# First feed-forward projection as Strassen products: seven half-width products for every two output pairs, and tile pools per phase

## The chip, the cores and the metric

The kernel runs on one core of a Trainium2 chip. The metric is device time in microseconds (us); 1770.32 us before the change is the median of three runs (1770.07 to 1771.31). The engines named below are TensorE (PE in the profile, with its weight loads as PEld), VectorE (DVE), ScalarE (ACT), GpSimd (POOL) and SyncE (SP), whose queue issues most loads.

## The reference

Two identical decoder layers on 512 tokens of width 1024, all in float32. A layer first adds the output of four causal token mixers (forgetting attention, gated linear attention, retention, a state-space scan) that share one input projection; then it adds a gated feed-forward block. The change lies in the latter:

```python
def swiglu(h, w_in, w_out):
    gate, up = jnp.split(h @ w_in, 2, axis=-1)
    return (jax.nn.silu(gate) * up) @ w_out

for l in range(DEPTH):                       # 2 layers
    h = rms_norm(x, ln1[l])
    x = x + mixer_block(h, ...)
    h = rms_norm(x, ln2[l])
    x = x + swiglu(h, w_ffn_in[l], w_ffn_out[l])
```

`w_ffn_in` is 1024 x 5632 (2816 gate columns, then 2816 up columns), `w_ffn_out` is 2816 x 1024.

## The kernel before

**Layout.** Activations are kept transposed: 128 features on the partitions, 512 tokens along the row. `x` has `KD` = 8 such tiles. The hidden width of 2816 is `NF` = 22 blocks of 128. A weight block is 128 x 128. A matmul takes a weight block as its stationary operand and 512 tokens as its moving one, and fills one PSUM bank of 128 x 512.

**Three passes.** Float32 accuracy comes from splitting every operand into a rounded high part (float32r) and a low part, what the rounding left. `mm3` (L164) issues three matmuls for one product: high by high, low weights by high moving, high weights by low moving. `split` (L175) makes the parts: a ScalarE copy rounds to the high part (L176), and a VectorE subtraction gives the low part (L177). All of these matmuls are recorded at L162.

**Weights.** They are packed on the host in the order of use, eight blocks to a slab of 128 x 1024 (512 KB). `load` puts a slab's transfer on SyncE's queue into `wr` (two buffers); `convert` splits it into `wh` and `wl` (three buffers each). `block` hands out the next block and calls `ahead`, which keeps `AHEAD` = 2 slabs prepared. In the program every slab is loaded once.

**Order.** The kernel is written in the Tile language: the program lists operations, and a scheduler places them on the engines' queues by a simulated timeline, with waits and buffer slots worked out from the data flow. An engine executes its own queue in order. In the mixers, pieces of the projections (`fill`) are mixed by hand with the mixers' own small matmuls. One pool `tp` of 37 tiles (128 x 512 float32, tag `t`) serves all temporary values of the whole kernel, in mixers and feed-forward alike.

**Feed-forward.** After the mixers' output projection, `resid` adds each result to `x` (L1155) and feeds the norm `n2`: `Norm.feed` makes the high and low part of `x` times the norm's gain, and sums of squares. The factor 1/rms per token, `n2.r`, is not in these parts; it is applied behind the projection. The block then runs in two halves (`hf`) of 11 blocks each. In the first half `group` computes the first two gate and up pairs, four columns at once in the four `mx` banks, while the last tiles of `x` come in; the other pairs come from `proj`, one column at a time, into four `mm` banks. `swiglu` multiplies gate and up by `n2.r` (L1175, L1176, VectorE), applies Silu (ScalarE), multiplies them (L1178, GpSimd) and splits the product. Then the half's 11 blocks go through `w_ffn_out`: four output columns together, then four one at a time, and `done` adds each to `x`: a plain addition after the first half (L1198), `resid` after the second, with the next layer's norm or the store of the output (L1159).

## Time and profile before

| what | value |
|---|---|
| median of three runs | 1770.32 us |
| profiled execution: its own time | 1771.39 us |
| profiled execution: span, first to last instruction | 1769.70 us |
| TensorE clock granted (mean) | 0.999 |
| instructions | 21568 |
| bytes moved by DMA | 163.31 MB |
| time share of DMA queue q1, all 16 engines | 27.5% |

The span is 1.69 us shorter than that execution's own time. Busy times in the profile are sums over an engine's instructions with overlaps counted once, except in the rows of groups, where each instruction counts in full: matmuls overlap there, since each one's time holds its latency, and the step from one start to the next is the shorter number. In rows of groups, `mm<-xh,wl` is a matmul into a `mm` bank with `xh` moving and `wl` stationary; `x128` is the count; behind the bar stand busy us, mean ns of one, and idle time ahead with its releaser.

### The profile page before, as it was taken

How to read it: one execution, taken by the hardware profiler on the slowest of the kernel's cores; microseconds unless marked ns; L12 is line 12 of the kernel's file. 1: busy time of each engine (PE TensorE's matmuls, PEld its weight loads, DVE VectorE, ACT ScalarE, POOL GpSimd, SP SyncE). 2: the span in 40 equal slices, each digit the busy share in tenths (PEclk: the TensorE clock that was granted, in tenths of full speed). 3: DMA queues.
4: the chain of work that ended last, by engine and by line, in shares of the span. 5: the costliest groups of instructions: out<-in, count | busy, mean ns of one | idle time of the engine just before them, and what ended most of it. 6: DMA issues, size and time to landing. Idle time of an engine off the chain costs nothing.

```text
span 1769.7 us, 21568 instructions
## 1 busy us (share of the span) xinstructions
PE 1760.0 (99%) x8700; PEld 1463.6 (83%) x8700; DVE 1041.5 (59%) x1427; ACT 684.8 (39%) x926; POOL 230.3 (13%) x210
## 2 busy tenths in 40 slices
PE   8999999999999999999999999999999999999999
PEld 7878888888888888888888788888888888888887
DVE  5866675777674443444447676867775644334442
ACT  5424543555443321223324254345554432223221
POOL 2032120022101110011000321201220111001100
PEclk9999999999999999999999999999999999999999
DMA  5322222222232222222323222222222323222222
GB/s 188 108 72 72 73 84 77 91 84 84 93 98 95 96 95 96 96 97 95 107 84 107 72 73 71 84 84 84 95 79 84 103 96 101 98 95 96 95 96 95
DMA packets 46036, 163.31 MB, mean 92 GB/s; under 512 B 5104, under 2 KB 5488, under 8 KB 45936
## 3 DMA queue, kind: packets, MB, share of 16 engines
q1 hardware_dynamic: 45072, 160.45, 27.5%
q10 hardware_dynamic: 864, 1.48, 0.3%
q8 instruction: 68, 1.11, 0.3%
q14 instruction: 32, 0.26, 0.1%
HBM read 159.81 MB, written 2.10 MB: 91 GB/s over the span
## 4 chain that ended last, share of the span: by engine, by line
PE 98%; ACT 0%; DVE 0%; DMA 0%; issue 0%; DVEq 0%; ACTq 0%
PE mm L162 83%; PE mx L162 14%; PE mx L1033 1%; DMA x<-in_x_dram 0%; PE mx L633 0%; DVE xl L355 0%; DVE t L367 0%; ACT xh L200 0%; ACT t L200 0%; PE mx L905 0%; PE mx L825 0%; DVE wl L177 0%; ACT wh L176 0%; ACT L195 0%; PE mx L621 0%
## 5 line engine op out<-in xcount | busy, mean ns | idle before, releaser
L176 ACT CAST wh<-wr 128x1024 fp32r<-128x1024 f32 (+1 forms) x300 | 313.1, 1045 | 737.8 <-PE mm L162 599.5
L162 PE MATMUL mm<-xh,wl 128*128 128x512 f32 x1504 | 589.2, 392 | 0.0
L162 PE MATMUL mm<-xh,wh 128*128 128x512 f32 x1504 | 589.1, 392 | 0.0
L162 PE MATMUL mm<-xl,wh 128*128 128x512 f32 x1504 | 588.1, 391 | 0.0
L177 DVE TENSOR_TENSOR wl<-wr,wh 128x1024 fp32r<-128x1024 f32 (+1 forms) x300 | 409.9, 1366 | 285.6 <-ACT wh L176 284.6
L162 PE MATMUL mm<-t,wh 128*128 128x512 f32 x1152 | 367.5, 390 | 0.0
L162 PEld LDWEIGHTS mm<-xh,wh 128*128 128x128 f32 x1504 | 282.5, 188 | 58.9 <-issue 1.3
L162 PEld LDWEIGHTS mm<-xl,wh 128*128 128x128 f32 x1504 | 282.5, 188 | 58.9 <-issue 1.3
L162 PEld LDWEIGHTS mm<-xh,wl 128*128 128x128 f32 x1504 | 282.6, 188 | 58.5 <-issue 1.1
L162 PEld LDWEIGHTS mm<-t,wh 128*128 128x128 f32 x1152 | 216.4, 188 | 44.7
L162 PE MATMUL mm<-t,wl 128*128 128x512 f32 x576 | 224.8, 390 | 0.0
L1178 POOL TENSOR_TENSOR t<-t,t 128x512 f32<-128x512 f32 x44 | 56.8, 1290 | 538.6 <-DVE t L1176 467.4
L162 PEld LDWEIGHTS mm<-t,wl 128*128 128x128 f32 x576 | 108.2, 188 | 22.0
L176 ACT CAST t<-t 128x512 fp32r<-128x512 f32 x112 | 68.7, 621 | 88.5 <-POOL t L1178 42.0
L177 DVE TENSOR_TENSOR t<-t,t 128x512 fp32r<-128x512 f32 x112 | 78.2, 704 | 29.6 <-ACT t L176 22.9
L1176 DVE TENSOR_TENSOR t<-mm,t 128x512 f32<-128x512 f32 x40 | 27.7, 691 | 115.0 <-PE mm L162 115.0
L200 ACT ACTIVATE t<-t 128x512 f32<-128x512 f32 x121 | 73.7, 628 | 24.2 <-DVE t L1175 14.5
L1126 POOL TENSOR_TENSOR t<-t,t 128x512 f32<-128x512 f32 x32 | 43.6, 1361 | 249.1 <-DVE t L1122 243.7
L162 PE MATMUL mx<-t,t 64*128 64x128 f32 (+6 forms) x576 | 63.8, 290 | 0.0
L1175 DVE TENSOR_TENSOR t<-mm,t 128x512 f32<-128x512 f32 x40 | 27.6, 691 | 61.1 <-PE mm L162 61.1
L162 PEld LDWEIGHTS mx<-t,t 128*128 128x128 f32 (+3 forms) x576 | 50.5, 165 | 14.2 <-issue 8.0
L162 PE MATMUL mx<-xh,wl 128*128 128x512 f32 x128 | 50.7, 400 | 3.0 <-DVE wl L177 3.0
(210 smaller groups left out, 1661.2 us busy)
## 6 DMA issues: line engine op xcount, KB each, us to landing
wr<-in_wst_dram SPq DMA_DIRECT2D x296, 512.0 KB, 3.3
out_dram<-x SPq DMA_DIRECT2D x8, 256.0 KB, 2.4
x<-in_x_dram SPq DMA_DIRECT2D x3, 512.0 KB, 6.3
wr<-in_wst_dram SPq DMA_DIRECT2D x4, 256.0 KB, 5.9
x<-in_x_dram SPq DMA_DIRECT2D x2, 256.0 KB, 5.4
cs<-in_cst_dram ACTq DMA_DIRECT2D x1, 462.0 KB, 5.9
pr<-in_par_dram ACTq DMA_DIRECT2D x2, 167.0 KB, 5.1
posi<-in_pos_dram ACTq DMA_DIRECT2D x1, 256.0 KB, 6.8
```

What stands on the lines that cost most here:

```text
L162: T.matmul(o, lhsT=l, rhs=r, start=start, stop=stop, skip_group_check=True)
L176: A.copy(out=hi, in_=src)
L177: V.tensor_tensor(out=lo, in0=src, in1=hi.bitcast(F32), op=ALU.subtract)
L200: i = A.activation(out=out, in_=in_, func=func, **kw)
L1033: T.transpose(ps[:, W:W + P], zs[qb][:, kb * P:(kb + 1) * P], ident)
L1126: (V if last else G).tensor_tensor(out=merged[d], in0=merged[d], in1=t, op=ALU.add)
L1175: V.tensor_tensor(out=a, in0=pg, in1=n2.r, op=ALU.mult)
L1176: V.tensor_tensor(out=u, in0=pu, in1=n2.r, op=ALU.mult)
L1178: G.tensor_tensor(out=a, in0=a, in1=u, op=ALU.mult)
```

## The change

The first projection of 20 of the 22 block pairs is computed by Strassen's scheme (in Winograd's form). A unit is two neighbouring blocks, each with its gate and its up column; for gate and up alike the 2 x 2 scheme runs over two output blocks, two halves of the contraction (`HK` = 4 tiles each) and two halves of the tokens (`H` = 256). Instead of eight quarter products there are seven, each 2 (gate, up) x 4 x 3 matmuls of 256 columns. They accumulate in three pairs of PSUM banks `a`, `b`, `c`, and ScalarE copies and VectorE sums (`collect`) put the four quarters of gate and up together.

The token sums t1 to t4 are made once per layer by `sums`, called inside the plain group that computes the first two pairs as before. The weight sums are made on the chip for every unit: `load` fetches four quarters (three into a new pool `rq`, one into `wr`), `prep` makes sums and splits three products ahead on VectorE and ScalarE. For three products that use a weight quarter as it is (`LATE`), the low part is made otherwise: ScalarE writes the negated rounded value, and an accumulating transfer on GpSimd's queue adds the weights from memory a second time (`early`).

The feed-forward block now runs in four parts (`PARTS` = 6, 6, 6, 4 blocks), each with its units and then its share of `w_ffn_out`. `swiglu` works on gate and up of two blocks at once (128 x 1024) and multiplies only the gate by `n2.r`; the up side's factor moves into `done`, which has two VectorE operations. The product of gate and up moves from GpSimd to VectorE. `mm3` issues high by high, high weights by low moving, low weights by high moving. Pools are opened and closed per phase: the mixers have 33 temporary tiles, the norms four of their own (`NT`), and the feed-forward phase its own pools in the same memory. `sbd` is cleared once per layer. `cap` keeps slabs from being prepared past the end of a phase.

The diff, cut to its core:

```diff
+    def mixers():
+        return phase(gp=2, vp=2, bd=1, tp=33)
...
     def mm3(o, l, r, start, stop):
         (lh, ll), (rh, rl) = l, r
         mm(o, lh, rh, start, False)
-        mm(o, ll, rh, False, False)
-        mm(o, lh, rl, False, stop)
+        mm(o, lh, rl, False, False)
+        mm(o, ll, rh, False, stop)
...
+        scope = phase(tq=1, ep=8, rp=5, lp=2, fp=9)
 
         last = l == DEPTH - 1
+        tb_ = {n: tuple(pools["tq"].tile([P, HK, H], F32R, tag=n + h, name=nm(n + h)) for h in "hl") for n in ("t1", "t2", "t3")}
+        tb_["t4"] = n2.hi[:, :HK, H:], n2.lo[:, :HK, H:]
+        tb_["b11"] = n2.hi[:, :HK, :H], n2.lo[:, :HK, :H]
+        tb_["b21"] = n2.hi[:, HK:, :H], n2.lo[:, HK:, :H]
+        tb_["b22"] = n2.hi[:, HK:, H:], n2.lo[:, HK:, H:]
+
...
+        def sums():
+            g = PR("ln2")
+            xg = []
+            for k in range(0, KD, 2):
+                t = FT([P, 2, S])
+                for i in range(2):
+                    act(out=t[:, i], in_=x[:, k + i], func=AF.Copy, scale=g[:, k + i:k + i + 1])
+                xg.append(t)
+            one_, two = slice(0, H), slice(H, S)
+
+            def make(n, f):
+                t = FT([P, HK, H])
+                for i in range(2):
+                    a, b = f(i)
+                    V.tensor_tensor(out=t[:, 2 * i:2 * i + 2], in0=a, in1=b, op=ALU.subtract)
+                split(t, *tb_[n])
+                return t
+
+            t1 = make("t1", lambda i: (xg[i][:, :, two], xg[i][:, :, one_]))
+            t2 = make("t2", lambda i: (xg[2 + i][:, :, two], t1[:, 2 * i:2 * i + 2]))
+            make("t3", lambda i: (xg[2 + i][:, :, two], xg[i][:, :, two]))
+            make("t4", lambda i: (xg[2 + i][:, :, one_], t2[:, 2 * i:2 * i + 2]))
+
+        RIGHT = {1: "b11", 2: "b21", 3: "b22", 4: "t4", 5: "t1", 6: "t2", 7: "t3"}
+        LATE = (1, 2, 4)
+        OF = {1: "11", 2: "12", 4: "22"}
+
+        def strassen(units):
+            n = len(units)
+            st = [{} for _ in units]
+            stream = [(0, 1), (0, 2)]
+            for u in range(n):
+                if u == n - 1 and u:
+                    stream += [(u, p) for p in (6, 5, 7, 2, 3, 4)]
+                else:
+                    stream += [(u, 6)] + ([(u, 2)] if u else []) + [(u, 5), (u, 7)]
+                    stream += [(u + 1, 1)] if u < n - 1 else []
+                    stream += [(u, 3), (u, 4)]
+            def load(u):
+                for q, (dk, dm) in (("11", (0, 0)), ("12", (HK, 0)), ("21", (0, 1)), ("22", (HK, 1))):
+                    if q == "22":
+                        t = wp.tile([P, SLAB * P], F32, tag="wr", name=nm("wr"), bufs=2)
+                    else:
+                        t = pools["rp"].tile([P, SLAB * P], F32, tag="rq", name=nm("rq"))
+                    j = len(qkeys) // SLAB
+                    for base in (0, FFN):
+                        qkeys.extend([("w_ffn_in", l, k + dk, base + (units[u] + dm) * P) for k in range(HK)])
+                    nc.sync.dma_start(out=t, in_=wsq[j])
+                    st[u][q] = t, j
+
+            def sub(o, a, b, op=ALU.subtract):
+                V.tensor_tensor(out=o, in0=a, in1=b, op=op)
+                return o
+
+            def LT():
+                return pools["lp"].tile([P, SLAB * P], F32R, tag="l", name=nm("l"))
+
+            def early(u, p):
+                t, j = st[u][OF[p]]
+                lo = wp.tile([P, SLAB * P], F32R, tag="wl", name=nm("wl"))
+                A.activation(out=lo, in_=t, func=AF.Copy, scale=-1.0)
+                G.dma_start(out=lo, in_=wsq[j], accum_op=ALU.add)
+                st[u]["lo", p] = lo
+
+            def prep(u, p):
+                s = st[u]
+                hi = wp.tile([P, SLAB * P], F32R, tag="wh", name=nm("wh"))
+                if p in LATE:
+                    A.copy(out=hi, in_=s[OF[p]][0])
+                    s[p] = hi, s.pop(("lo", p))
+                    return
+                a11, a12, a21, a22 = (s[q][0] for q in ("11", "12", "21", "22"))
+                if p == 6:
+                    s1 = wp.tile([P, SLAB * P], F32, tag="wr", name=nm("wr"), bufs=2)
+                    s["s1"] = sub(s1, a21, a22, ALU.add)
+                    sub(a21, a11, a21)
+                    sub(a11, s1, a11)
+                    s[p] = split(a11, hi, LT())
+                    if u + 1 < len(units):
+                        load(u + 1)
+                    return
+                if p == 3:
+                    sub(a12, a12, a11)
+                t = {5: s["s1"], 7: a21, 3: a12}[p]
+                s[p] = split(t, hi, LT())
+
...
+            def begin(i):
+                if i < 0:
+                    load(0)
+                    upto("early", 2, early, lambda p: p in LATE)
+                    return
+                upto("prep", i + 3, prep, lambda p: True)
+                upto("early", i + 6, early, lambda p: p in LATE)
+
+            def product(u, p):
+                s = st[u]
+                hi, lo = s.pop(p)
+                if p in (1, 2, 5):
+                    s["abc"[(1, 2, 5).index(p)]] = [MM(), MM()] if p == 1 else [MX(), MX()]
+                bank = s["b" if p == 2 else "c" if p in (3, 5) else "a"]
+                rh, rl = tb_[RIGHT[p]]
+                for g in range(2):
+                    for k in range(HK):
+                        sl = slice((HK * g + k) * P, (HK * g + k + 1) * P)
+                        mm3(bank[g][:, :H], (hi[:, sl], lo[:, sl]), (rh[:, k], rl[:, k]), p in (1, 2, 5) and k == 0, k == HK - 1)
+
+            def collect(u, p, have):
+                s = st[u]
+                left, right = slice(0, H), slice(H, S)
+
+                def copy(n):
+                    for g in range(2):
+                        s[n, g] = pools["ep"].tile([P, H], F32, tag="e", name=nm("e"))
+                        A.copy(out=s[n, g], in_=s["a"][g][:, :H])
+
+                def plus(n, bank, i, cols):
+                    for g in range(2):
+                        V.tensor_tensor(out=s["t"][g][:, i, cols], in0=s[bank][g][:, :H], in1=s.pop((n, g)), op=ALU.add)
+
+                if p in (1, 6, 7):
+                    copy({1: "e1", 6: "e2", 7: "e3"}[p])
+                if "t" not in s and p != 1:
+                    s["t"] = [FT([P, 2, S]), FT([P, 2, S])]
+                if p == 2:
+                    plus("e1", "b", 0, left)
+                if p == 7:
+                    plus("e3", "c", 1, right)
+                if p == 3:
+                    plus("e2", "c", 0, right)
+                if p == 4:
+                    for g in (1, 0):
+                        A.copy(out=s["t"][g][:, 1, left], in_=s["a"][g][:, :H])
+                    swiglu(*s.pop("t"))
+            def run():
+                for i, (u, p) in enumerate(stream):
+                    begin(i)
+                    if i >= len(stream) - 2:
+                        ahead(len(keys) // SLAB + AHEAD - len(stream) + 1 + i)
+                    product(u, p)
+                    collect(u, p, None)
+                assert done_["prep"] == len(stream)
+
...
+        def swiglu(a, u):
+            V.tensor_tensor(out=a, in0=a, in1=n2.r.unsqueeze(1).broadcast_to([P, 2, S]), op=ALU.mult)
+            act(out=a, in_=a, func=AF.Silu)
+            V.tensor_tensor(out=a, in0=a, in1=u, op=ALU.mult)
+            hi, lo = split(a, FT([P, 2, S], F32R), FT([P, 2, S], F32R))
+            acts.extend((hi[:, i], lo[:, i]) for i in range(2))
+
...
-            def swiglu(pg, pu):
-                a, u = TT(), TT()
-                V.tensor_tensor(out=a, in0=pg, in1=n2.r, op=ALU.mult)
-                V.tensor_tensor(out=u, in0=pu, in1=n2.r, op=ALU.mult)
-                act(out=a, in_=a, func=AF.Silu)
-                G.tensor_tensor(out=a, in0=a, in1=u, op=ALU.mult)
-                acts.append(split_tile(a))
...
+        def hook():
+            sums()
+            begin(-1)
+
+        ps4 = group("w_ffn_in", l, [0, FFN, P, FFN + P], n2, KD, hook)
...
+        for part, n in enumerate(PARTS):
+            end = part == len(PARTS) - 1
+            cap[0] = len(keys) // SLAB + n + (FRONT // SLAB if end and not last else 0)
+            run()
+            if end and not last:
                 o, w = PAR_OFF["ln1"]
                 nn = Norm(pr[:, l + 1, o:o + w])
+            k0 = sum(PARTS[:part])
 
             def done(ps, d):
-                if hf == 0:
-                    V.tensor_tensor(out=x[:, d], in0=ps, in1=x[:, d], op=ALU.add)
-                else:
-                    resid(ps, d, nn)
-
-            ps4 = [MM() for _ in range(4)]
-            for k in range(HF):
+                t = FT([P, 2, S])[:, 0]
+                V.tensor_tensor(out=t, in0=ps, in1=n2.r, op=ALU.mult)
+                V.tensor_tensor(out=x[:, d], in0=x[:, d], in1=t, op=ALU.add)
+                if end and not last:
+                    nn.feed(d)
+                elif end:
+                    nc.sync.dma_start(out=out[:, d], in_=x[:, d])
+
+            ps4 = [MX() for _ in range(4)]
+            for k in range(n):
                 for i in range(4):
-                    mm3(ps4[i], block("w_ffn_out", l, hf * HF + k, P * i), acts[k], k == 0, k == HF - 1)
+                    mm3(ps4[i], block("w_ffn_out", l, k0 + k, P * i), acts[k], k == 0, k == n - 1)
+            if not end:
+                begin, run = ready_for(part + 1)
+                begin(-1)
             for i in range(4):
                 done(ps4[i], i)
             for d in range(4, KD):
                 ps = MM()
-                for k in range(HF):
-                    mm3(ps, block("w_ffn_out", l, hf * HF + k, P * d), acts[k], k == 0, k == HF - 1)
+                for k in range(n):
+                    mm3(ps, block("w_ffn_out", l, k0 + k, P * d), acts[k], k == 0, k == n - 1)
                 done(ps, d)
+            acts.clear()
```

More of the change, by code (lines that the diff above doesn't have):

```diff
@@ L206, in trunk @@
     raw, ready = [], []
+    cap = [SLABS]
     def load():
@@ L257, in wide @@
         return hi[:, sl], lo[:, sl]
+    scope = mixers()
     x = cp.tile([P, KD, S], F32, name="x")
@@ L399, in proj, with layer @@
         return ps
-    def layer(l, n1):
+    def layer(l, n1, scope):
+        sbd = pools["bd"].tile([P, 7, 2, P], F32, name=nm("sbd"))
+        G.memset(sbd, 0.0)
+        gp, vp = pools["gp"], pools["vp"]
+        cap[0] = len(keys) // SLAB + FRONT // SLAB
         def PR(n):
@@ new lines, in layer, with ready_for @@
+        acts = []
+        def swiglu(a, u):
[4 more added lines that the diff above has]
+            acts.extend((hi[:, i], lo[:, i]) for i in range(2))
+        def ready_for(n):
+            m = PLAIN if n == 0 else sum(PARTS[:n])
+            return strassen(list(range(m, sum(PARTS[:n + 1]), 2)))
@@ new lines, in layer @@
+        nn = None
+        begin, run = ready_for(0)
+        def hook():
+            sums()
+            begin(-1)
+        ps4 = group("w_ffn_in", l, [0, FFN, P, FFN + P], n2, KD, hook)
+        n2.rstd()
+        a, u = FT([P, 2, S]), FT([P, 2, S])
+        for i in range(2):
+            V.tensor_tensor(out=a[:, i], in0=ps4[2 * i], in1=n2.r, op=ALU.mult)
+            A.copy(out=u[:, i], in_=ps4[2 * i + 1])
+        act(out=a, in_=a, func=AF.Silu)
+        V.tensor_tensor(out=a, in0=a, in1=u, op=ALU.mult)
@@ L1221, in trunk @@
     for l in range(DEPTH):
-        n1 = layer(l, n1)
-    assert len(keys) == SLABS * SLAB, (len(keys), SLABS * SLAB)
+        n1 = layer(l, n1, scope if l == 0 else mixers())
+    assert len(keys) == SLABS * SLAB and len(qkeys) == QUADS * SLAB, (len(keys), SLABS * SLAB, len(qkeys), QUADS * SLAB)
 def _params(inp):
```

77 lines of the change are left out of this document (44 added, 33 removed).

## The prediction

> **What bounds the kernel now.** I read the page's busy table first, then TensorE's waits, then the chain in order of time, then groups and short stretches of the timeline.
>
> ```profile
> PE 1760.0 (99%) x8700; PEld 1463.6 (83%) x8700; DVE 1041.5 (59%) x1427; ACT 684.8 (39%) x926; POOL 230.3 (13%) x210
> PEclk9999999999999999999999999999999999999999
> ...
> PE mx L162 <- DVE wl L177: 3.0, 2, 2.6
> PE mx L162 <- ACT wh L176: 1.6, 2, 1.4
> PE mm L162 <- POOL t L285: 1.4, 1, 1.4
> ...
> 281.85 11.60 PE mm L162 x96
> 530.88 21.76 PE mx L162 x96
> 552.63 337.76 PE mm L162 x1490
> 1406.48 21.76 PE mx L162 x96
> 1428.24 337.77 PE mm L162 x1490
> ```
>
> TensorE is busy 99% at full clock, and all its waits come to 6.0 us, at the start. The last five rows are the chain: one feed-forward layer is 21.76 us (the four-column group) plus 337.76 us of matmuls without a gap, 1584 in all and two for the norm. So a saving here is a saving in matmul pitch, and every new wait counts in full.
>
> The pitch is read from the same rows. A 512-column matmul takes 21.76 / 96 = 0.2267 us and 337.76 / 1490 = 0.2267 us, start to start. The row of 281.85 is a token-major projection; these are the groups in that window (count, then busy us and mean ns of one):
>
> ```profile
> L162 PE MATMUL mm<-wh,xh 128*128 128x256 f32 x32 | 9.1, 286 | 0.0
> L162 PE MATMUL mm<-wh,xl 128*128 128x256 f32 x32 | 9.1, 283 | 0.0
> L162 PE MATMUL mm<-wl,xh 128*128 128x256 f32 x32 | 9.1, 283 | 0.0
> ```
>
> So 96 matmuls of 256 columns take 11.60 us: 0.1208 each. (The 283 ns are latency, which overlaps.) From the two pitches a column costs (226.7 - 120.8) / 256 = 0.4137 ns and each matmul some 15 ns beside its columns. That 15 ns is what the change pays for.
>
> **The change part by part.**
>
> *Seven products (the gain).* Of 22 block pairs in a layer, 2 stay plain; 20 become 10 units of two pairs. Before, a unit was 2 x 2 x 8 x 3 = 96 matmuls of 512 columns: 21.76 us. After, it is 7 x 2 x 4 x 3 = 168 of 256 columns: 168 x 0.1208 = 20.30 us. In parts: 12.5% fewer columns, 6144 x 0.4137 ns = 2.54 us gained, and 72 x 15 ns = 1.08 us paid. The gain is 1.46 us a unit, 29.2 us for 20 units. It would be nothing at a pitch of 21.76 / 168 = 0.1295 us. Number and shape of the second projection's 528 matmuls stay.
>
> The Trainium skill, TensorE: Matmul & The Clock Gate, section Back-to-back issue gap, states an isolated gap of N / 2.4 + 2.5 ns. By it the unit's gain would be 2.37 us and the time about 1732 us. The trace does not agree: both pitches lie some 11 ns above it (226.7 against 215.8, 120.8 against 109.2), so the rows decide.
>
> *VectorE and ScalarE per unit.* A 1024-wide tensor operation runs at 1.23 us, one every 1.14 us, when nothing is against it:
>
> ```profile
> 565.12 1.23 DVE L177 TENSOR_TENSOR wl<-wr,wh 128x1024 fp32r<-128x1024 f32 x1 [2.17 <-ACT wh L176]
> 566.26 0.69 DVE L177 TENSOR_TENSOR t<-t,t 128x512 fp32r<-128x512 f32 x1
> 566.86 0.68 DVE L1175 TENSOR_TENSOR t<-mm,t 128x512 f32<-128x512 f32 x1
> 567.46 0.68 DVE L1176 TENSOR_TENSOR t<-mm,t 128x512 f32<-128x512 f32 x1
> ...
> 586.63 1.29 POOL L1178 TENSOR_TENSOR t<-t,t 128x512 f32<-128x512 f32 x1 [9.59 <-DVE t L1176]
> 586.92 2.08 DVE L177 TENSOR_TENSOR wl<-wr,wh 128x1024 fp32r<-128x1024 f32 x1 [0.44 <-ACT wh L176]
> ...
> L176 ACT CAST wh<-wr 128x1024 fp32r<-128x1024 f32 x296 | 310.8, 1051 | 737.8 <-PE mm L162 599.5 <-issue 64.1 <-PE mx L162 59.7
> L816 ACT COPY t<-mx 64x256 f32<-64x256 f32 x8 | 2.5, 364 | 0.0
> ```
>
> VectorE gets per unit four operand sums (s1, two in place, a12 - a11), four low parts, and in `swiglu` two products and a low part: 11 x 1.14 = 12.5 us, and six 256-wide sums from PSUM at about half of the 0.60 us step, 1.9 us: 14.4 of 20.3 us. ScalarE gets three negated casts, seven high parts, a Silu and a cast, 12 x 1.05 = 12.6 us, and eight 256-wide copies at 0.364: 15.5 us. Both fit with a quarter to spare; the price is zero while they keep two products (5.8 us) ahead, which is how far `prep` runs. Moving the gate product (L1178) off POOL also takes away the overlap that made the subtraction 2.08 us.
>
> *Order within those queues.* Behind the last product of a unit stands the chain of `collect(4)`: two copies, product, Silu, product, cast, subtraction: 0.28 (matmul's end) + 2 x 0.364 + 1.23 + 1.05 + 1.23 + 1.05 + 1.23 = 6.8 us, and six handovers of some 0.05, so 7.1. If the engines kept the program's order, the next product's cast would queue behind this cast and its subtraction end about 8.0 us after the unit's end, due at 2 x 24 x 0.1208 + 0.24 = 6.0: 2.0 us lost at each of 12 boundaries between units (6 a layer), 24 us. If the scheduler pulls the cast forward into ScalarE's idle time, nothing. The trace shows that it does not keep the program's order: in the middle of one projection's 24 matmuls stand two of a head norm.
>
> ```profile
> 302.52 0.39 PE L162 MATMUL mm<-xl,wh 128*128 128x512 f32 x1
> 302.75 0.62 PE L162 MATMUL mx<-t,cr 128*128 128x512 f32 x2
> 303.21 0.40 PE L162 MATMUL mm<-xh,wh 128*128 128x512 f32 x1
> ```
>
> I take a value near that end, 0.3 us x 12 = 3.6 us, and keep 0 and 24.
>
> *From products to the second projection.* In parts of 6 blocks, four earlier blocks (4 x 12 x 0.2267 = 10.9 us) cover the 7.1 us chain. In the last part of 4, two blocks cover 5.4 us, and the low half is due one matmul later, 5.7: 1.4 us lost, 2.9 us in two layers. Bounds: 0 (matmuls of another column pulled forward) to 2 x 3.
>
> *Start of the first unit.* `hook` adds to the plain group eight scaled copies, eight half-sums and four splits for t1 to t4, and the first unit's operands. The group's window before, and the second layer's:
>
> ```profile
> core 0: us, PE busy (x) PEld busy (x) DVE busy (x) ACT busy (x) POOL busy (x), PEclk, DMA share, GB/s
> 530.88:552.63 21.75, 21.75 (x97) 18.02 (x97) 7.64 (x8) 5.91 (x7) 1.78 (x1) 1.00 0.29 97
> 552.63:890.39 337.76, 337.76 (x1492) 279.74 (x1491) 154.85 (x156) 102.87 (x124) 31.58 (x24) 1.00 0.30 97
> 1406.00:1428.00 22.00, 22.00 (x99) 18.23 (x98) 7.64 (x8) 5.92 (x7) 1.78 (x1) 1.00 0.31 104
> ```
>
> VectorE: 7.6 + 8 x 0.60 + 4 x 1.14 + 4 x 1.14 for the first product with sums = 21.5 us, due 5.8 us after the group's 21.75 us. It fits with 6 us over, but it hangs on x's last column and on loads into memory that the mixers have just left. I take 1 us a layer, 2 us; bounds 0 and 6. The group's four PSUM tiles are freed by two copies for product 2 and, after the norm's root, by two products for product 5 (8.7 us on): hidden.
>
> *Loads.* SyncE's queue still loads each weight once (2 MB a unit), and waits there now for slots of `rq` and `wr`; behind a waiting load stand only later loads, one unit ahead. New is POOL's queue: three accumulating transfers of 512 KB a unit, each behind a ScalarE cast, none with a row here. The nearest:
>
> ```profile
> POOL 2032120022101110011000321201220111001100
> q1 hardware_dynamic: 45072, 160.45, 27.5%
> wr<-in_wst_dram SPq DMA_DIRECT2D x296, 512.0 KB, 3.3
> ```
>
> 160.45 MB in 27.5% of 1769.7 us is 330 GB/s when busy: 1.59 us of the 16 engines for 512 KB. A unit's four loads take 6.4 us and three accumulating transfers 4.8 us at the plain price, 9.5 at double (they read their target too): 16 of 20.3 us. They are issued five products (14.5 us) ahead against 3.3 us to land, so I take zero; from 2.9 times the plain price on (14 us) the DMA engines set the pace, which is the other end.
>
> The Trainium skill, DMA: Bandwidth & Descriptors, section Anatomy of one DMA, puts a GpSimd-issued transfer at 2.0 us plus bytes / 436 GB/s: 3.2 us as an estimate here, hidden. The Trainium skill, SBUF — State Buffer, section Who interferes with whom, speaks against such transfers: GpSimd cannot write their descriptors while VectorE runs a two-port mode. The same section excepts `tensor_tensor`, nearly all that VectorE runs beside them here; no run here shows either.
>
> *Small parts.* `done` has one more VectorE operation, which shows only at the kernel's end, between the last matmul and the store:
>
> ```profile
> 1765.61 0.39 PE L162 MATMUL mm<-t,wh 128*128 128x512 f32 x1
> 1766.04 0.69 DVE L1155 TENSOR_TENSOR x<-mm,x 128x512 f32<-128x512 f32 x1 [6.79 <-PE mm L162]
> 1766.76 0.33 SPq L1159 DMA_DIRECT2D out_dram<-x  x1
> ```
>
> 0.7 us. It is done in four rounds instead of two, but VectorE has room (154.85 of 337.76 us). The mixers' pool goes from 37 to 33 tiles, with four for the norms apart: TensorE waits for none of these today; 0.5 us, bounds 0 and 6. `sbd` is cleared once more, on a POOL that is idle there, long before its first use: zero. `mm3` asks for the moving low part before the weights' low part: up to the 3.0 us quoted at the start, taken as zero.
>
> *The sum.* The profiled execution took 1771.39 us (span 1769.70, 1.69 around it). 1771.39 - 29.2 + 3.6 + 2.9 + 2.0 + 0.7 + 0.5 = 1751.9. The median of the three runs is 1.07 lower, so 1751 us. Without any wait it would be 1742.
>
> **The rivals.**
>
> *The queues keep their order* at the unit boundaries: 24 us instead of 3.6, 1771 us, about the time before. For it: both engines go from under half busy to three quarters, and the chain is longer than the two products that cover it. Against it: the interleaving shown above.
>
> *The accumulating transfers set the pace (slower than before).* It decides at 21.76 - 6.4 = 15.4 us for three, 5.1 us of all DMA engines each, 3.2 times the plain price. At four times a unit takes 6.4 + 19.1 = 25.5 us, 3.7 more than before, and the kernel 1770 + 20 x 3.7 + 6 = 1850 us. For it: no such transfer is in this trace, and POOL must write the descriptors. Against it: it takes a price three times the plain one.
>
> *A 256-column matmul doesn't keep 0.1208 us* for 60 us on end: weight loads double in rate with it. At 0.133 us a unit is 22.3 us, and the kernel 1770 + 20 x 0.6 + 10 = 1792 us. For it: PEld is busy 83% now. Against it: 96 such pairs ran at that pitch.
>
> **How the numbers follow.** Forecast 0.66 (waits of 0 to 20 us in all: its own range is 1741 to 1762), queue order 0.18 (1764 to 1778), transfers 0.09, pitch 0.07. The range 1739 to 1779 holds the first two and the mild end of the others; its low end is the sum without waits, 1742, with the 0.1200 us that a shorter stretch could give. Faster by over 0.2% (3.5 us, about what a measurement here tells from none): 0.66, and 0.06 of queue order and 0.02 of milder transfers: 0.74. Same: 0.07. Slower: 0.19.
>
> **What would show it.** Each product's 24 matmuls in 2.90 us; a unit in 20.3; TensorE's waits under 15 us in sum, none longer than 2, most on the chain to the second projection of the last part; two-input VectorE operations at 1.23 us; the accumulating transfers landing within 10 us. The prediction is wrong if TensorE waits at unit boundaries for `wh` or `l` (queue order), for `wl` (transfers), or if the products' matmuls run at over 0.125 us with nothing waited for.

## The result, and the profile after

The changed kernel takes 1751.3 us (median of four runs, 1750.9 to 1751.86) against 1770.64 us for the kernel before on the same chip (four runs): a ratio of 0.9891, 95% interval 0.9874 to 0.9908. The forecast was 1751 us. The number came out almost to the microsecond, but not by the terms of the sum: two of them were too pessimistic and one loss was missing altogether. One of the five executions of the kernel `b_shift` below took 3583.28 us, twice the others, for a reason that stays open, and is left out of its time.

The page of the changed kernel, its busy row, its DMA rows and the landing time of the accumulating transfers:

```profile
PE 1736.9 (99%) x10140; PEld 1500.2 (86%) x10140; DVE 1215.5 (69%) x1683; ACT 862.0 (49%) x1190; POOL 225.9 (13%) x227
...
q1 hardware_dynamic: 45072, 160.45, 29.0%
q0 software_dynamic: 8640, 31.46, 10.4%
```

```profile
wl<-in_wsq_dram POOLq DMA_DIRECT2D x60, 512.0 KB, 5.7
```

1440 more matmuls and TensorE is still busy 99%: it remains the bound. VectorE went from 59% to 69%, ScalarE from 39% to 49%.

What TensorE waits for in the changed kernel (total us, times, longest):

```profile
PE mm L183 <- DVE wl L198: 2.6, 6, 0.4
PE mx L183 <- ACT wh L197: 2.3, 3, 1.1
PE mm L183 <- POOL t L308: 1.4, 1, 1.4
PE mx L183 <- DVE t L198: 1.1, 2, 0.6
PE mm L183 <- DVE t L1147: 0.8, 2, 0.4
```

8.2 us in sum, against 6.0 before; the first row is the only new wait in the feed-forward layers. Where it sits comes with the experiment on its cause.

The chain of the changed kernel in order of time (start, length, what):

```profile
507.54 22.40 PE mm L183 x96
529.94 16.34 PE mx L183 x72
...
592.17 16.80 PE mx L183 x72
...
657.88 8.56 PE mm L183 x72
```

Divide length by count. The rows are, in this order, a token-major projection of the mixers (512 columns, `t` moving), the plain group (512 columns, `xh` or `xl` moving), a second projection (512 columns, `f` moving) and three products (256 columns): 0.2333, 0.2269, 0.2333 and 0.1189 us. The last is better than the 0.1208 of the prediction. The first and third should be 0.2267, as the same groups were before: **every 512-column matmul of the projections whose moving operand is `t` or `f` has become 3% slower**, with the clock at 1.00 and nothing waited for. No step of the prediction had that.

The two feed-forward layers and what lies between them, in the view of stretches (columns: length; busy us and count of PE, PEld, DVE, ACT, POOL; granted clock; DMA share; GB/s):

```profile
529.90:877.00 347.10, 345.79 (x2308) 316.03 (x2307) 239.21 (x279) 192.10 (x256) 28.91 (x32) 1.00 0.57 144
877.00:1397.70 520.70, 519.59 (x2754) 431.67 (x2753) 364.41 (x555) 237.36 (x336) 83.69 (x77) 1.00 0.27 86
1397.70:1744.80 347.10, 345.79 (x2306) 316.02 (x2305) 238.58 (x279) 184.62 (x246) 27.15 (x31) 1.00 0.57 144
```

Before, the same three stretches were 359.5, 516.1 and 359.3 us. From the starts of the matmuls that bound them:

| stretch | before | after | difference |
|---|---|---|---|
| up to the first feed-forward layer | 530.71 | 529.78 | -0.9 |
| feed-forward, first layer | 359.52 | 347.19 | -12.3 |
| mixers, second layer | 516.09 | 520.74 | +4.65 |
| feed-forward, second layer | 359.29 | 347.13 | -12.2 |
| behind the last matmul | 4.05 | 4.92 | +0.9 |
| span | 1769.66 | 1749.76 | -19.9 |

The mixers, whose computation did not change, got slower, and a layer gained 12.3 us where ten units at 1.46 us and the predicted waits gave 10.4.

### The profile page after: what moved, and what is told of

Its sections match the earlier page's. It is cut to its first block, busy times and chain, and to the rows that moved or that the text cites. A ratio compares the mean times of both kernels' runs of the same rounds, so it can differ in the third digit from the quotient of the medians.

```text
span 1749.8 us, 25123 instructions
## 1 busy us (share of the span) xinstructions
PE 1736.9 (99%) x10140; PEld 1500.2 (86%) x10140; DVE 1215.5 (69%) x1683; ACT 862.0 (49%) x1190; POOL 225.9 (13%) x227
## 3 DMA queue, kind: packets, MB, share of 16 engines
q0 software_dynamic: 8640, 31.46, 10.4%
## 4 chain that ended last, share of the span: by engine, by line
PE 96%; DVE 2%; DMA 1%; ACT 1%; issue 0%; ACTq 0%; DVEq 0%
PE mm L183 64%; PE mx L183 31%; DVE wl L198 1%; PE mx L1058 0%; DMA x<-in_x_dram 0%; DMA t<-in_ext_dram 0%; ACT wh L197 0%; DVE f L1399 0%; DVE x L1400 0%; PE mx L658 0%; DVE t L352 0%; ACT L216 0%; ACT g L221 0%; DVE t L1147 0%; PE mx L930 0%
## 5 line engine op out<-in xcount | busy, mean ns | idle before, releaser
L183 PE MATMUL mm<-xh,wh 128*128 128x512 f32 (+1 forms) x1184 | 431.4, 364 | 0.8 <-DVE t L1147 0.8
L183 PE MATMUL mm<-xh,wl 128*128 128x512 f32 (+1 forms) x1184 | 430.5, 364 | 0.0
L183 PE MATMUL mm<-xl,wh 128*128 128x512 f32 (+1 forms) x1184 | 429.8, 363 | 0.0
L198 DVE TENSOR_TENSOR wl<-wr,wh 128x1024 fp32r<-128x1024 f32 (+1 forms) x220 | 282.0, 1283 | 117.9 <-ACT wh L197 109.7
L183 PE MATMUL mm<-t,wh 128*128 128x512 f32 x448 | 142.5, 397 | 0.0
L183 PE MATMUL mx<-xl,wh 128*128 128x256 f32 (+1 forms) x448 | 140.4, 313 | 0.0
L183 PE MATMUL mx<-xh,wh 128*128 128x256 f32 (+1 forms) x448 | 137.8, 314 | 2.3 <-ACT wh L197 2.3
L183 PE MATMUL mx<-f,wh 128*128 128x512 f32 x352 | 110.2, 395 | 0.0
L183 PEld LDWEIGHTS mm<-t,wh 128*128 128x128 f32 x448 | 83.2, 188 | 19.1
L183 PE MATMUL mm<-t,wl 128*128 128x512 f32 x224 | 88.5, 395 | 0.0
```

The source lines that it names most:

```text
L183: T.matmul(o, lhsT=l, rhs=r, start=start, stop=stop, skip_group_check=True)
L198: V.tensor_tensor(out=lo, in0=src, in1=hi.bitcast(F32), op=ALU.subtract)
```

## The experiments

**Two candidates for the slower pitch, tried in the kernel before: the order in `mm3`, and the tiles' addresses.** The change turned round the last two matmuls of `mm3`. It also moved the tiles: by the compiled kernels' addresses, all matmul operands before start at 64 modulo 128 bytes in their partition; after the change `t`, `f`, `t1` to `t3`, `l` and `rq` start at 0, the weights `wh`, `wl` and the activations `xh`, `xl` still at 64. The first kernel does the order alone, the second shifts the kernel before's `tp` by 64 bytes.

```diff
 # b_order: the kernel before, mm3
-        mm(o, ll, rh, False, False)
-        mm(o, lh, rl, False, stop)
+        mm(o, lh, rl, False, False)
+        mm(o, ll, rh, False, stop)
```

> The kernel before with only the new order inside mm3 (high weights by high moving, high weights by low moving, low weights by high moving). Theory A (the slower 512-column pitch after the change, 0.2333 us where f or t moves, comes from the place of the tiles in memory): that pitch stays at 0.2267; the two waits for wl at the start (3.0 us) and the eight matmuls at half clock behind the longer one (8 x 0.2 = 1.6 us) go, so about 4.5 us faster, 1766 us. Theory B (the slower pitch comes from this order): some 2030 matmuls with t moving go to 0.2333, 13.5 us, minus 4.5: about 1779 us.

Measured: 1768.68 us against 1770.17 (ratio 0.9991, 0.9982 to 1.0001), and matmuls with `t` moving stay at 227 ns. The order is not the cause. Of the 4.5 us expected at the start 1.5 came by the medians: the longer wait for `wl` shrank from 2.6 to 1.5 us, but TensorE now waited 2.3 us for `wh` ahead of the first projection, and the eight matmuls behind that wait ran at a granted clock of 0.53.

```diff
 # b_shift: the kernel before, ahead of the pool tp
+    pd = ctx.enter_context(tc.tile_pool(name="pd", bufs=1))
...
+    G.memset(pd.tile([P, 16], F32, name="pad"), 0.0)
```

> The kernel before with only a pad of 64 bytes per partition in front of the pool of temporary tiles, so that t starts at 0 instead of 64 modulo 128 bytes, as t and f do after the change (wh, wl, xh and xl stay at 64). Theory A (place in memory): the 2030 matmuls of 512 columns with t moving go from 0.2267 to 0.2333 us, 13.5 us slower, 1784 us; those with xh or xl moving keep 0.2267. Theory B (order in mm3): no change, 1770 us, pitch 0.2267 everywhere.

Measured: 1777.79 us (ratio 1.0041, 1.0027 to 1.0056). An addition of 64 unused bytes costs 7.6 us by the medians. The chain shows it: the same stretch of 1490 matmuls that took 337.77 us before, and an `mx` group with `xh` moving that did not change.

```profile
531.82 21.81 PE mx L163 x96
...
1432.53 339.04 PE mm L163 x1490
```

The direction is the one expected, the size about half: matmuls with `t` moving and `wh` as weights went to 231 ns, those with `wl` hardly moved (226), where the changed kernel has 233 for both.

**The addresses, put right in the changed kernel.** Three kernels: all pools of the phases shifted by 64 bytes, so that everything starts at 64; only those of `tp` and `fp` (the moving operands `t` and `f`), so that the products keep `l` and t1 to t3 at 0; and everything shifted, so that the difference between the operands stays while each one's own place changes.

```diff
 # a_align: the changed kernel, one pad behind the pool sp, so ahead of all pools of the phases
+    pd = ctx.enter_context(tc.tile_pool(name="pd", bufs=1))
...
+    G.memset(pd.tile([P, 16], F32, name="pad"), 0.0)
 # a_mixed: the changed kernel, in phase()
+            if n in ("tp", "fp"):
+                pad = st.enter_context(tc.tile_pool(name=nm("pd"), bufs=1, reuse_waits="tile"))
+                G.memset(pad.tile([P, 16], F32, name=nm("pad")), 0.0)
 # a_cp64: the changed kernel, in the first pool
+    G.memset(cp.tile([P, 16], F32, name="pad"), 0.0)
```

> The changed kernel with only a pad of 64 bytes ahead of the phase pools, so that t, f, t1 to t3, rq and l start at 64 modulo 128 like the weights. Theory A (place in memory): 2030 matmuls of 512 columns with t or f moving go from 0.2333 to 0.2267 us, 13.5 us less; the products with t1 to t3 moving or l as weights go from 0.118 to 0.120, 3.8 us more: about 1742 us. Theory B (order in mm3): no change, 1751 us.

> The changed kernel with two pads of 64 bytes, ahead of the mixers' tile pool and ahead of the feed-forward tile pool alone: t and f start at 64 modulo 128 like the weights wh and wl; t1 to t3 and l stay at 0. By the pitches read so far (512 columns: 227 ns when moving tile and weights start alike, 233 when not; 256 columns: 120 alike, 118 when not) it keeps the gain of the pad in front of all pools (7.4 us) and adds 20 units x 96 matmuls x 2 ns = 3.8 us: 1740 us. If what matters is something else than the two start addresses modulo 128, 1744 us or more.

> The changed kernel with 64 bytes more in the first pool: every later tile moves by 64, so wh, wl, xh and xl start at 0 modulo 128 and t, f, t1 to t3 and l at 64. If the difference between the moving tile's and the weights' start matters, all pitches stay (233 for t and f, 227 for xh, 118 and 120 for the products) and the time is 1751 us. If the moving tile's own start matters (64 good for 512 columns), t and f go to 227 and xh to 233: 2976 x 6.3 ns more, 2030 x 6.5 ns less, about 1757 us.

| kernel | t, f moving (512) | products (256), mean | median us | ratio (95%) |
|---|---|---|---|---|
| changed | 233 ns | 118.6 ns | 1751.3 | 0.9891 (0.9874 to 0.9908) |
| a_align | 227 | 120.0 | 1743.91 | 0.9852 (0.9837 to 0.9866) |
| a_mixed | 227 | 118.6 | 1739.6 | 0.9824 (0.9809 to 0.9838) |
| a_cp64 | 233 | 118.6 | 1751.73 | 0.9893 (0.9876 to 0.9909) |

Pitches go from start to start: medians over all 512-column matmuls of a kind, and the mean over the 3360 of the products without the steps over 160 ns, which hold waits. The chain of a_mixed has the same three kinds of row as the changed kernel's:

```profile
505.67 21.76 PE mm L186 x96
...
589.66 16.35 PE mx L186 x72
...
654.50 8.56 PE mm L186 x72
```

22.40 became 21.76, 16.80 became 16.35, and the products' 8.56 stayed. So the loss is one of placement: shifting `t` and `f` alone by 64 bytes removes it, and shifting them together with the weights leaves it as it is (a_cp64), so that the difference between the two starts counts and not each one's own place. At 512 columns the difference of 64 costs 6 ns a matmul. At 256 columns it pays: where all operands start alike, the mean is 120.0 ns (a_align), and 118.6 where some start 64 bytes from the others. That gain doesn't go by a matmul's own two operands: `t1` to `t3` moving with `l` as weights start alike and take 118 ns like the rest of their products, and `xh` moving with `l` takes 113 between others of 120. In the changed kernel 1056 matmuls with `f` and 864 with `t` moving stood on the wrong side: 1920 x 6.5 ns = 12.5 us by pitch, 11.7 us by the medians of the changed kernel and a_mixed.

**What the seven products are worth by themselves.** The 20 pairs computed plainly, without the token sums and the weight sums, everything else of the change kept: parts, pools, `swiglu`, `done`, order in `mm3`.

```diff
 # a_plain: the changed kernel, in run()
...
-                    product(u, p)
-                    collect(u, p, None)
+                for u in units:
+                    t = [FT([P, 2, S]), FT([P, 2, S])]
+                    for i in range(2):
+                        for g, base in enumerate((0, FFN)):
+                            A.copy(out=t[g][:, i], in_=proj("w_ffn_in", l, base + P * (u + i), n2, KD))
+                    swiglu(*t)
```

> The changed kernel with the 20 pairs computed plainly (24 matmuls of 512 columns for each column, copies to the same 128 x 1024 tiles, the same swiglu, parts and pools; no token sums, weight sums or accumulating transfers). It isolates the seven products. By the term of the prediction (1.46 us a unit) it takes 29 us more than the changed kernel, 1780 us; by the pitch that the changed kernel's trace shows (0.1187 us, 1.82 us a unit) 36 us more, 1788 us, less up to 2 us of waits that the weight sums bring.

Measured: 1783.44 us (ratio 1.0076, 1.0061 to 1.0091). The products give 32.1 us net, and what surrounds them costs 13 us net. The placement accounts for 12 of that by the pitch above, and what else was lost and got back nearly cancels (a feed-forward layer is 363.1 us here, 3.6 above before; 528 matmuls at 6.5 ns are 3.4). In its chain the second projection is as slow as in the changed kernel while the plain products beside it are at the old pitch (the 360 of the second row are 72 more of the second projection at 0.2333 and 288 plain ones, which leaves these 0.2267):

```profile
595.87 16.80 PE mx L183 x72
612.66 82.10 PE mm L183 x360
```

**The queues at a unit's boundary.** The first rival was that ScalarE keeps the program's order, so that the next product's cast stands behind the chain of `swiglu`. Here that order is made binding for the first such cast after each `swiglu`, on ScalarE alone.

```diff
 # a_tied: the changed kernel; tied[0] is prep's cast, tied[1] the cast of the swiglu before it
+            def tie():
+                if tied[1] is not None:
+                    order(tied[0], tied[1])
+                    tied[1] = None
...
-                    A.copy(out=hi, in_=s[OF[p]][0])
+                    tied[0] = A.copy(out=hi, in_=s[OF[p]][0])
+                    tie()
...
```

> The changed kernel with one edge more for the scheduler: after every swiglu, the first high-part cast of prep comes behind the cast in that swiglu on ScalarE, as in the program's order. It prices the rival of the queue order. By the prediction's working 2.0 us are lost at each of 12 boundaries between units, 24 us in all: 1775 us. If the two products of lead cover more than that working says, or the queues stand in that order already, under 5 us: 1751 to 1756.

Measured: 1757.39 us (ratio 0.9925, 0.991 to 0.994), 6.1 us over the changed kernel. A feed-forward layer takes 349.95 and 349.77 us, 2.7 more: some 0.65 us at four of the six boundaries, 0.2 or less at the other two. The mechanism is real and was over-priced: 2.0 us were worked out for each boundary, 24 in all. ScalarE's timeline at one such boundary, first in the changed kernel, then in this one:

```profile
649.11 1.05 ACT L221 ACTIVATE f<-f 128x1024 f32<-128x1024 f32 x1
650.07 1.03 ACT L197 CAST wh<-wr 128x1024 fp32r<-128x1024 f32 x1
...
653.95 1.05 ACT L197 CAST f<-f 128x1024 fp32r<-128x1024 f32 x1
```

```profile
649.13 1.05 ACT L223 ACTIVATE f<-f 128x1024 f32<-128x1024 f32 x1
...
652.10 1.05 ACT L199 CAST f<-f 128x1024 fp32r<-128x1024 f32 x1 [0.70 <-DVE f L1372]
653.06 1.04 ACT L199 CAST wh<-wr 128x1024 fp32r<-128x1024 f32 x1
```

The scheduler had put the weights' cast (`wh`) into the time between Silu and the cast of `swiglu` (`f`); tied, it comes 3 us later, and still only some 0.65 us of that reaches TensorE.

**The accumulating transfers, replaced by VectorE.** The low part of the three `LATE` products is made by a subtraction, as all others are.

```diff
 # a_noaccum: the changed kernel, prep (early does nothing)
-                    A.copy(out=hi, in_=s[OF[p]][0])
-                    s[p] = hi, s.pop(("lo", p))
+                    s[p] = split(s[OF[p]][0], hi, wp.tile([P, SLAB * P], F32R, tag="wl", name=nm("wl")))
```

> The changed kernel with the low parts of the three plain weight quarters made as everywhere else, by a VectorE subtraction from the tile that is already there, without the negated cast and the accumulating transfer. Three operations more on VectorE, 3 x 1.14 = 3.4 us a unit: 17.8 of some 19.9 us; ScalarE has 3.2 us less. If VectorE's slack hides it: 1751, within 2 us. If its queue is full at the unit boundaries, up to 1 us a unit: 1771. Without the transfers a wait for them would go, but the trace shows none.

Measured: 1757.34 us (ratio 0.9924, 0.991 to 0.9939), 6.0 us slower. The same stretch of products, first the changed kernel's, then this one's:

```profile
637.00:686.00 49.00, 49.00 (x416) 49.00 (x415) 35.16 (x41) 30.47 (x44) 3.45 (x4) 1.00 0.75 185
```

```profile
637.00:686.00 49.00, 48.56 (x408) 48.16 (x407) 42.13 (x46) 26.92 (x40) 0.00 (x0) 1.00 0.33 105
```

VectorE goes from 72% to 86% and TensorE gets through 408 matmuls instead of 416, while the DMA engines drop from 0.75 to 0.33. So the transfers take work off VectorE for DMA time that nobody else needs, and they are worth 6 us net, small as that is beside 32. That VectorE's load is what costs the 6 us is a reading and not shown: what TensorE waits for here are ScalarE's casts and copies, some of which wait for VectorE's sums in turn.

```profile
PE mx L183 <- ACT wh L197: 4.8, 11, 1.7
PE mm L183 <- ACT e L1320: 2.1, 2, 1.0
PE mm L183 <- ACT wh L197: 1.7, 8, 0.2
```

The changed kernel's row for `wl` is missing among these, which bears on the next question: during the second projection nothing but the slabs asks for a tile of `wl` here. The price of the transfers can be read from the changed kernel's page: 10.4% of 16 engines over 1749.8 us is 182 us for 60, 3.03 us each of all DMA engines, 1.9 times the plain 1.59.

**The wait for `wl`.** The changed kernel's six waits lie in the second projection, three a layer, one in each of the first three parts, within the sixth output column, where a new slab begins. VectorE beside the first of them:

```profile
613.22 0.69 DVE L1399 TENSOR_TENSOR f<-mm,n 128x512 f32<-128x512 f32 x1 [1.30 <-PE mm L183]
613.94 0.69 DVE L1400 TENSOR_TENSOR x<-x,f 128x512 f32<-128x512 f32 x1
614.67 1.23 DVE L198 TENSOR_TENSOR wl<-wr,wh 128x1024 fp32r<-128x1024 f32 x1
```

The subtraction that TensorE waits for stands behind `done`'s two operations. One reading: VectorE is late because `done` has an operation more. The other: the subtraction cannot run earlier because `wl` has three buffers, of which two are already held by the early low parts of the next part's first products. The first kernel gives the addition to GpSimd, the second asks for those low parts behind the sixth and the seventh output column instead of ahead of the fifth. Both are made on a_mixed.

```diff
 # a_pooladd: a_mixed, done
-                V.tensor_tensor(out=x[:, d], in0=x[:, d], in1=t, op=ALU.add)
+                (V if end else G).tensor_tensor(out=x[:, d], in0=x[:, d], in1=t, op=ALU.add)
 # a_slots: a_mixed; begin(-2) only loads; the early low parts follow in the loop over output columns
+                if not end and d in (5, 6):
+                    begin(2 - d)
```

> The kernel with the two pads (1739.6 us), where in addition the second operation of done, the addition to x, runs on GpSimd in the first three parts instead of VectorE. The trace shows TensorE waiting some 0.7 us in each of those six second projections for a slab's low part whose subtraction stands on VectorE behind done. If that queue is the cause, the waits go: about 1736 us. If GpSimd's additions hold up VectorE's two-input operations as the multiplications did before the change (0.85 us each), the low part comes no sooner: 1739 to 1743 us.

> The kernel with the two pads (1739.6 us), with the two low parts for the next part's first products asked for later: after columns 5 and 6 of the second projection instead of ahead of column 0 to 3's additions. Moving the additions to GpSimd made the wait longer, and there the subtraction waits for TensorE, so the theory now is the slots of wl: three, two of them held by those early low parts while the second projection needs two for its slabs. If so, the six waits of 0.7 us go and the products that use the low parts still have them in time: 1735 to 1736 us. If the slots are not the cause: 1740, or more if the first products now wait for their transfers (5.7 us to land, 8.3 us of cover).

a_pooladd: 1743.24 us (ratio 0.9844, 0.9829 to 0.9858), 3.6 slower than a_mixed; the waits grew.

```profile
PE mm L186 <- DVE wl L201: 6.6, 6, 1.4
```

```profile
611.21 1.80 DVE L201 TENSOR_TENSOR wl<-wr,wh 128x1024 fp32r<-128x1024 f32 x1 [0.66 <-PE mm L186]
```

VectorE was idle for 0.66 us ahead of that subtraction and was released by a matmul, not by `done`, which is how it would be if it waited for TensorE to finish with a buffer of `wl`. (It takes 1.80 us instead of 1.23 while GpSimd's addition runs beside it, from 610.64 us on.) a_slots: 1733.91 us against 1771.34 (ratio 0.9791, 0.9775 to 0.9808), 5.7 faster than a_mixed, and the row for `wl` is gone from TensorE's waits, which are now all in the mixers:

```profile
PE mx L186 <- ACT wh L200: 2.6, 3, 1.3
PE mm L186 <- POOL t L311: 1.4, 1, 1.4
PE mx L186 <- DVE t L201: 1.2, 2, 0.6
PE mm L186 <- DVE t L1150: 0.9, 2, 0.5
```

So it was the buffers: a_noaccum, which holds none of them ahead, lacks that wait too. A feed-forward layer is 341.4 us here, 18.1 under before: ten units at the 1.83 us that the pitch gives, less 0.2 us in all. This is the fastest kernel of the study, 2.1% under before.

**The order in `mm3`, put back in the changed kernel.** This was to tell whether order and address act together on the pitch.

```diff
 # a_oldorder: the changed kernel, mm3
-        mm(o, lh, rl, False, False)
-        mm(o, ll, rh, False, stop)
+        mm(o, ll, rh, False, False)
+        mm(o, lh, rl, False, stop)
```

> The changed kernel with the order inside mm3 put back (high by high, low weights by high moving, high weights by low moving). If the slower 512-column pitch of t and f needs both, another start modulo 128 than the weights' and the new order, it goes from 233 to the mean of 231, 231 and 227 that the shifted old kernel shows, 229.7 ns: 1920 x 3.7 = 7.1 us less, minus 1.5 to 2.5 us that the new order saves at the start: about 1746 us. If the start alone sets it: 1753 us.

Measured: 1756.51 us against 1771.25 (ratio 0.9918, 0.9901 to 0.9934). The expectation missed: matmuls with `t` and `f` stay at 233 ns, the second projection at 16.80 / 72, and the kernel is 5.2 us slower by the medians, 5.0 by the spans.

```profile
592.17 16.80 PE mx L183 x72
```

```profile
593.90 16.80 PE mx L183 x72
```

(The changed kernel's row, then this one's.) What it costs are waits. In the feed-forward layers, 3.2 us longer together, the low part of the weights is asked for one matmul earlier, and the row for `wl` goes from 2.6 us to the first row below. Another 1.2 us lie ahead of the first feed-forward layer, most of them at the start, where a wait of 2.07 us for `wh` is followed by nine matmuls in 3.37 us (second row, clock 0.54):

```profile
PE mm L183 <- DVE wl L198: 4.7, 6, 0.8
...
7.67:11.04 3.37, 3.37 (x9) 2.60 (x10) 2.26 (x4) 3.34 (x6) 0.17 (x1) 0.54 1.02 405
```

Why a shift of 64 bytes in the kernel before gave 231 and 226 ns with the two weight parts, and 233 with both in the changed kernel, stays open: the order does not explain it. One candidate is untested: by the compiled kernels' addresses, the moving tile's start less that of the weights is 64 modulo 512 bytes in b_shift and 448 in the changed kernel, which are the same only modulo 128. So the period of the effect is not shown.

## Why the prediction was right, point by point

**The gain of the seven products: sign and mechanism right, size too small.** A product's 24 matmuls took 2.85 us, not 2.90; a unit 168 x 0.1186 = 19.93 us, not 20.30; the gain is 1.83 us a unit, 36.6 us for 20, not 29.2. The step that failed is the pitch from 96 / 11.60: the first step of that window, out of neighbouring work, took 0.203 us, while the median pitch of those matmuls was 0.1200. That makes 20 x 168 x 0.00083 = 2.8 us of the difference. The rest is the placement again, this time as a gain: products with some operands 64 bytes apart ran at 0.1177 with t1 to t3 moving, and a_align, where all start alike, is 4.3 us slower than a_mixed. No step had that, so this part was luck. The rival "a 256-column matmul doesn't keep 0.1208" is dead. By the rule cited from the Trainium skill, TensorE: Matmul & The Clock Gate, section Back-to-back issue gap, 256 columns would be at 109.2 ns as an estimate; the products' mean of 118.6 stays 9 ns above it, so the rows were the better guide, though not by the whole of their distance.

**Waits in the feed-forward layers: 8.5 us predicted (3.6, 2.9 and 2.0), some 5 us measured, in another place.** From matmul to matmul a layer lost 2.4 and 2.5 us, 0.7 at each of three places and at no other more than 0.2: next to nothing at unit boundaries, at the entry to the last part and at the first unit. The prediction's sign for the transfers, a wait for `wl`, did appear, but on the low part of a slab that VectorE makes, not on a transfer. The three terms were each sized by the latency of one chain; the wait that came was one for buffers, and the prediction did not ask who holds `wl`.

**Queue order (0.18): the rival's condition never arose**, and a_tied, which binds ScalarE's order alone, puts its price at 6 us instead of 24.

**Accumulating transfers: right.** 5.7 us to land against the 14.5 us of lead that was worked out, 1.9 times the plain price where double was reckoned and 3.2 was the point of decision; DMA share 0.75 beside products where 16 of 20.3 us, 0.79, was worked out. VectorE's two-input operations stayed at 1.23 us beside them, and its load, 35.16 of 49 us, is the 14.4 of 20.3 that was summed. The exception for `tensor_tensor` that the prediction cited from the Trainium skill, SBUF — State Buffer, section Who interferes with whom, agrees with this; the same section has a two-input VectorE operation contend with a GpSimd instruction that reads SBUF, and a_pooladd's 1.80 us against 1.23 agrees too.

**The small parts.** The tail cost 0.9 us for 0.7. The mixers were given 0.5 us for both layers; by the table they and the start cost 3.7, of which the placement is 2 x 2.93 (a_mixed takes 517.8 us for the second layer's mixers, the changed kernel 520.7). The 3.9 us that the first stretch got back lie at the start, where `mm3`'s order was "up to the 3.0 us, taken as zero". The order alone is part of it: in b_order's profile the first feed-forward layer starts at 528.23 us instead of 530.71, 2.5 earlier. What brings the rest is not shown. The row of before and the one of after at the same place:

```profile
24.00:27.40 3.40, 3.40 (x8) 2.71 (x9) 2.62 (x3) 0.87 (x2) 0.33 (x1) 0.51 0.62 187
```

```profile
24.00:27.40 3.40, 3.40 (x17) 2.82 (x16) 1.79 (x3) 1.67 (x2) 0.56 (x1) 1.00 0.79 252
```

Before, the 2.6 us wait for `wl` was followed by eight matmuls at a clock of 0.51; after, with no wait over 1.1 us there, 17 fit into the same 3.4 us.

**What was not in the sum at all: the placement.** The prediction listed 37 to 33 tiles and pools in the same memory, priced their effect on waits and let every 512-column matmul keep 0.2267 us. "Number and shape of the second projection's matmuls stay" was true and not enough. The whole account, with each term from the runs:

| term | predicted | measured | from |
|---|---|---|---|
| seven products | -29.2 | -36.24 | a_slots less before, feed-forward: 18.12 + 18.12 |
| waits in the feed-forward layers | +8.5 | +5.57 | a_mixed less a_slots: 2.74 + 2.83 |
| `f` 64 bytes from the weights | 0 | +6.18 | changed less a_mixed, feed-forward: 3.05 + 3.13 |
| `t` 64 bytes from the weights | 0 | +5.86 | changed less a_mixed, second layer's mixers, doubled: 2 x 2.93 |
| mixers' pools, order and start | +0.5 | -2.14 | table of stretches, less the line above |
| tail | +0.7 | +0.87 | table of stretches |
| sum | -19.5 | -19.90 | span: -19.9 |

These are profiled executions; by the medians the difference is 19.3 us. The forecast was right by cancellation: 7.0 us of gain too few and 5.6 us of waits and start too many against 12.0 us of a loss that no step contained. That they cancelled was luck.

## What to carry to other kernels

When a change moves tiles, take the pitch of matmuls that it does not touch (chain row: length over count) before and after; 64 bytes of padding were worth 11.7 us here, a third of what the algorithm gave. Price a prefetch by the buffers it holds as well as by its lead: asking for two tiles of three earlier than needed cost 5.7 us here, paid by the work that wanted the third. And when a total agrees with the forecast, still check each term, for the next improvement lies in those that cancelled.

## What the hardware showed that was not expected

- The pitch of float32r matmuls depended on where their operands start in a partition, relative to each other: 512 columns took 227 ns with moving tile and weights at the same place modulo 128 bytes and 233 at 64 bytes apart (a_mixed, changed kernel); the products of 256 columns took 120.0 ns on average with all operands alike (a_align) and 118.6 with some 64 bytes apart. In the kernel before with a shifted `tp` the step was smaller (231 and 226), which stays unexplained.
- One wait of TensorE of 2.6 us (before), 2.3 us (b_order) or 2.07 us (a_oldorder) was followed by some 3.4 us at a granted clock of 0.51 to 0.54; behind one of 1.5 us (b_order) the clock stayed at 1.00.
- An accumulating transfer of 512 KB takes 3.03 us of all 16 DMA engines, 1.9 times a plain load, and lands in 5.7 us (7.0 in a_slots).
